# A two-block transformer kernel: first modulation columns loaded once, block 2's recurrence and norms rewritten, more buffers for the first query weights

## The chip, the cores and the metric

The kernel runs on one NeuronCore of a Trainium2 chip, as one launch. The metric is the device time of that launch in microseconds. Engines are named as in the profile: PE is TensorE's matmul, PEld its weight load, DVE VectorE, ACT ScalarE, POOL GpSimd, SP SyncE, which here only issues DMAs.

## What is computed

256 tokens `x` and 256 context tokens, 1024 wide, all fp32, pass a first block of two layers, a final norm, and a second block of one layer. Cut to what matters:

```python
for l in range(2):                                   # first block
    m_x = split6(silu(c) @ w_mod[l] + b_mod[l])      # shift, scale, gate, twice
    m_c = split6(silu(c_ctx) @ w_mod[l] + b_mod[l])
    h  = rmsnorm(x, g1) * (1 + m_x[1]) + m_x[0];  hc = same of ctx with m_c
    x  = x + m_x[2] * token_mix(h, kv of hc)         # attention, Fourier mix, pool mix
    h2 = rmsnorm(x, g2) * (1 + m_x[4]) + m_x[3]
    x  = x + m_x[5] * peer(h2)                       # 8 heads, top 16 of 128x128 experts
    if l == 0: ctx likewise
x = rmsnorm(x, final_g)
# second block
h = rmsnorm(x, norm1_g_2) * (1 + scale1) + shift1
x = x + gate1 * (attention(h), rwkv7_both_directions(h)) @ w_out
x = x + gate2 * peer(rmsnorm(x, norm2_g_2) * (1 + scale2) + shift2)
```

`peer` takes the 16 best of the sums of two key scores per head, so 128 experts for each token, reads the two 1024-wide rows of each expert, and adds the second, weighted with gelu of the token's product with the first.

## The kernel before

The program is first recorded and ordered, then issued. `Prog` (line 361) records every operation with the tile that it writes; `emit` (line 1803) writes the program down in segments (`x0`, `m0`, `p0`, `c0`, `q0` and so on), each with a span of due values in the table `ORDER`. `schedule` (line 558) then takes operations engine by engine, by what is ready, by priority (`lift` raises it) and due value, and assigns on-chip memory to tiles; a table `QUOTA` says how many buffers a tag (segment name and tile name, as `p0w`) may have at once. `replay` issues the result, so every operation stands at line 694 in the profile, and an edit of a number in a table can move operations everywhere. Each engine executes its own queue in order.

The streams, in the order of time: `x0` (first layer's mix of the tokens), `p0` (lookup and experts of the tokens), `c0` (mix of the context), `q0` (its experts), `x1` and `y1` (second layer's mix), `p1` (its experts), `b2` (final norm and block 2's mix), `p2` (its experts). The 256 tokens of an expert stage are two tiles of 128. For each tile 128 indirect DMAs on POOL fetch, for each of 128 tokens, one expert's two rows (8 KB, so 1.05 MB for a DMA, the `tab` transfers); DVE takes the products (`scalar_tensor_tensor` over 1024 columns with a running sum, and a `DVE_READ_ACCUMULATOR` behind it), ACT the gelu, and DVE or PE adds the weighted rows.

- Modulation. `load_c` (788) broadcasts `c`, applies silu; `mods` (795) loads a 128x1024 tile of transposed weights per column of 128 outputs and lets DVE multiply and sum it. `FIRST` is the list of the 16 columns that the first norm needs (8 scales, 8 shifts). At lines 1852 and 1856 they are loaded for `c`, and later again for `c_ctx`. `gscale` (817) makes (1 + scale) * g, eight operations of one column.
- Norms. `ln` (841): ACT squares, PE sums them with a matrix of ones, `rstd` (824) takes a logarithm and an exponential on ACT, DVE multiplies, ACT adds the shift. `final_norm` (1686) is followed by block 2's first `ln` (1923), both by token tile.
- Lookup. `select` loads query weights `wpq` (16 tiles of 0.5 MB) as tile `w` of its stream: `p0w` in the first.
- Recurrence. `wkv` (1551) is called for 4 groups of 2 heads in 2 directions. In chunks of 64 tokens, two to a tile `i`, it inverts a triangular matrix by five levels of products (line 1616), `Tm` and `XX` in turn, applies it to `Wr`, which gives `N`, and makes for each of four chunks the transition `GZ` and the input `HZ` of the state.

```python
1616            for lv in range(1, 6):
...
1638            nc.scalar.activation(N[:, i], px[:, :T].rearrange("p (e t) -> p e t", t=P), AF.Copy, scale=-1.0)
```

Of the kernel before, what the change touches and what calls it, by code (L numbers as in the profile page):

```python
# [17 lines left out]
OP = mybir.AluOpType  # L18
# [678 lines left out]
class Kern:  # L697
# [70 lines left out]
    def setup(self):  # L768
        nc, A = self.nc, self.A
        self.xT = self.t([P, KD, T], "xT", 1)  # L770
        self.cols = self.t([P, _NCOLS], "cols", 1)
        nc.sync.dma_start(self.xT, A["xT"])
        nc.sync.dma_start(self.cols, A["cols"])
        self.ident = self.t([P, P], "ident", 1)
        nc.sync.dma_start(self.ident, A["ident"])
        self.ones = self.t([P, P], "ones", 1)
        nc.vector.memset(self.ones, 1.0)
        self.eps = self.t([P, 4], "eps", 1)
        for i, v in enumerate((EPS, LNX_EPS, 0.0, 1.0)):
            nc.vector.memset(self.eps[:, i:i + 1], v)  # L780
        self.junk = self.t([P, D], "junk", 1, BF16)
        self.iota = self.t([P, P], "iota", 1)
        nc.gpsimd.iota(self.iota, pattern=[[1, P]], base=0, channel_multiplier=0,
                       allow_small_or_imprecise_dtypes=True)
        self.zero = self.t([P, 512], "zero", 1)
        nc.vector.memset(self.zero, 0.0)

    def load_c(self, dst, src):
        nc = self.nc
        nc.sync.dma_start(dst, src.to_broadcast([P, D]))  # L790
        s = self.t([P, D], "cs", 2)
        nc.scalar.activation(s, dst, AF.Sigmoid)
        nc.vector.tensor_tensor(dst, dst, s, op=OP.mult)

    def mods(self, wt, cols, outs, bufs=6):

        vec, left = self.nc.vector, {}
        for j in cols:
            left[j // 8] = left.get(j // 8, 0) + 1
        for j in cols:  # L800
            w = self.w(wt[j], "wm", bufs)
            left[j // 8] -= 1
            for m, cb, b in outs:
                vec.scalar_tensor_tensor(self.junk, w, 1.0, cb, op0=OP.mult, op1=OP.mult, accum_out=m[:, j:j + 1])
            if not left[j // 8]:
                c = slice(j // 8 * 8, j // 8 * 8 + 8)
                for m, cb, b in outs:
                    vec.tensor_tensor(m[:, c], m[:, c], b[:, c], op=OP.add)

# [7 lines left out]
    def gscale(self, m, j, g, name):  # L817
        r = self.t([P, KD], name, bufs=2)
        for k in range(KD):
            self.nc.vector.scalar_tensor_tensor(r[:, k:k + 1], m[:, j + k:j + k + 1], 1.0, g[:, k:k + 1],  # L820
                                                op0=OP.add, op1=OP.mult)
        return r
# [728 lines left out]
    def wkv(self, m, d, ld, a, R, Kf, kk, ka1, Vt, yT):  # L1551
# [29 lines left out]
        GZ = self.t([P, 4, 64], "GZ")  # L1581
        HZ = self.t([P, 4, 64], "HZ")
        te = [ch * 64 + (63 if d == 0 else 0) for ch in range(4)]
        ps = self.ps()
# [11 lines left out]
        for i in range(NT):  # L1596
# [18 lines left out]
            nc.vector.tensor_tensor(XX[:, :, 1], idb, al[:, 0], op=OP.subtract)  # L1615
            for lv in range(1, 6):
                px = self.ps()
# [5 lines left out]
                for e in range(2):  # L1623
                    if lv < 5:
                        nc.tensor.matmul(px[:, e, 0], XX[:, e, 1], Tm[:, e], start=True, stop=True)
                    nc.tensor.matmul(px[:, e, 1], Tm[:, e], XX[:, e, 1], start=True, stop=True)
                if lv < 5:
                    nc.vector.tensor_tensor(XX, XX, px, op=OP.subtract)
# [7 lines left out]
            for e in range(2):  # L1636
                nc.tensor.matmul(px[:, e * P:(e + 1) * P], XX[:, e, 1], Wr[:, i, e], start=True, stop=True)
            nc.scalar.activation(N[:, i], px[:, :T].rearrange("p (e t) -> p e t", t=P), AF.Copy, scale=-1.0)
            pr = self.ps()
# [9 lines left out]
            else:  # L1649
                nc.vector.tensor_tensor(yT[:, ts], pr[:, P:2 * P], yT[:, ts], op=OP.add)  # L1650
            pg = [self.ps() for _ in range(2)]
            for e in range(2):
                o = 64 * e
                for cc in range(2):
                    rs = slice(64 * cc, 64 * cc + 64)
                    nc.tensor.matmul(pg[cc][o:o + 64, :64], N[rs, i, e, :64], QKt[rs, 0, i, o:o + 64], start=True, stop=True)
                    nc.tensor.matmul(pg[cc][o:o + 64, 64:P], QKt[rs, 1, i, o:o + 64], Vt[rs, i, o:o + 64], start=True, stop=False)
                    nc.tensor.matmul(pg[cc][o:o + 64, 64:P], QKt[rs, 0, i, o:o + 64], N[rs, i, e, 64:], start=False, stop=True)
            for cc in range(2):
                ch = 2 * i + cc  # L1660
                nc.vector.tensor_tensor(GZ[:, ch], pg[cc][:, :64], self.id2, op=OP.add)
                nc.scalar.activation(HZ[:, ch], pg[cc][:, 64:P], AF.Copy, scale=Dc[:, te[ch]:te[ch] + 1])

        order = range(4) if d == 0 else range(3, -1, -1)
        Z = None
# [20 lines left out]
    def final_norm(self, xT, g):  # L1686
# [7 lines left out]
        nc.lift = self.lift  # L1694


FIRST = [j + k for k in range(KD) for j in (KD, 0)]
# [18 lines left out]
QUOTA = {  # L1716
# [78 lines left out]
ORDER.update({  # L1795
# [7 lines left out]
def emit(K, out, stage=None):  # L1803
# [45 lines left out]
    for q, n in zip(cbs, ("c", "c_ctx")):  # L1849
        K.load_c(q, A[n])  # L1850
    both = [(modx[0], cbs[0], bm[0]), (modc[0], cbs[1], bm[0])]
    K.mods(A["wmod0"], FIRST, both[:1])
    K.load_mix(0)
    h = norm1(xT, modx[0], 0)
    K.kvproj(0, h, T, True)
    K.mods(A["wmod0"], FIRST, both[1:])
    hc = K.ln(cT, K.gscale(modc[0], 8, n1[0], "gsc"), modc[0][:, 0:8], name="c")
# [54 lines left out]
    if stage == "peer1":  # L1912
        return dump(xT)
    K.final_norm(xT, K.col("final_g"))
    if stage == "first":
        return dump(xT)
    block2(K, out, stage, m2)


def block2(K, out, stage, m2):  # L1920
    nc, A, xT = K.nc, K.A, K.xT
    K.begin("b2", {"ps": 6, "pt": 2}, "b2", "p1s")
    h = K.ln(xT, K.gscale(m2, 8, K.col("norm1_g_2"), "gsc"), m2[:, 0:8], spans=TILES)
    if stage is None:
# [184 lines left out]
```

## Time and profile before

| | |
|---|---|
| runs | 3940.00, 3948.54, 3950.16 us; median 3948.54 |
| profiled execution | 3951.66 us, span 3949.7 us |
| granted TensorE clock | 0.887 of full speed |
| busy | PE 2966.0 (75%), PEld 1760.1, DVE 2858.3 (72%), ACT 1992.4 (50%), POOL 1485.3 us |
| DMA | 1314.31 MB, mean 333 GB/s |

The profile is of one execution. Busy times are shares of the whole span; the span has stages with different limits, so the rows below are mostly of single stretches. In a row of a timeline the brackets hold the idle time of that engine just before and what released it; in a grouped row stand count, busy time, mean length of one in ns, and idle time. A fp32 matmul leaves two rows, xN counts rows.

### The profile page before, as it was taken

How to read it: one execution, taken by the hardware profiler on the slowest of the kernel's cores; microseconds unless marked ns; L12 is line 12 of the kernel's file. 1: busy time of each engine (PE TensorE's matmuls, PEld its weight loads, DVE VectorE, ACT ScalarE, POOL GpSimd, SP SyncE). 2: the span in 40 equal slices, each digit the busy share in tenths (PEclk: the TensorE clock that was granted, in tenths of full speed). 3: DMA queues.
4: the chain of work that ended last, by engine and by line, in shares of the span. 5: the costliest groups of instructions: out<-in, count | busy, mean ns of one | idle time of the engine just before them, and what ended most of it. 6: DMA issues, size and time to landing. Idle time of an engine off the chain costs nothing.

```text
span 3949.7 us, 40304 instructions
## 1 busy us (share of the span) xinstructions
PE 2966.0 (75%) x10928; PEld 1760.1 (45%) x10928; DVE 2858.3 (72%) x6792; ACT 1992.4 (50%) x6181; POOL 1485.3 (38%) x1165
## 2 busy tenths in 40 slices
PE   5998844787895699866789656656989989666655
PEld 4767511454561256522376212212666776322222
DVE  5964999767799965576678986665644439986666
ACT  4123655556556676566536667666424234433322
POOL 0001345344343544455113455552201213564454
PEclk8999976898998899998899888887988999988887
DMA  8843999999999999999779999997520118999998
GB/s 330 299 153 113 369 374 387 383 406 375 388 398 397 411 404 412 418 421 420 253 264 397 416 403 421 421 422 291 195 82 19 37 45 340 410 419 421 422 422 356
DMA packets 222274, 1314.31 MB, mean 333 GB/s; under 512 B 24608, under 2 KB 29152, under 8 KB 90720
## 3 DMA queue, kind: packets, MB, share of 16 engines
q0 software_dynamic: 147456, 1073.81, 66.4%
q1 hardware_dynamic: 74592, 237.93, 16.5%
q8 instruction: 88, 1.44, 0.1%
q14 instruction: 138, 1.13, 0.1%
HBM read 1310.59 MB, written 1.05 MB: 332 GB/s over the span
## 4 chain that ended last, share of the span: by engine, by line
DVE 24%; issue 20%; POOL 15%; PE 15%; DMA 14%; ACT 4%; POOLq 0%; DVEq 0%; SPq 0%; ACTq 0%
DVE sb L694 24%; POOL sb L694 15%; PE bank L694 15%; DMA sb<-in_tab_dram,sb 11%; ACT sb L694 2%; ACT L694 1%; DMA sb<-in_wada_dram 1%; DMA sb<-in_wmod_dram 1%; DMA sb<-in_wo_dram 1%; POOLq L694 0%; DMA sb<-in_win_dram 0%; DMA sb<-in_wpq_dram 0%; DVEq L694 0%; SPq L694 0%; DVEq L2104 0%
## 5 line engine op out<-in xcount | busy, mean ns | idle before, releaser
L694 PE MATMUL bank<-sb 128*128 128x256 f32 (+8 forms) x10928 | 2966.0, 428 | 977.4 <-ACT sb L694 907.7
L694 PEld LDWEIGHTS bank<-sb 128*128 128x128 f32 (+5 forms) x10928 | 1760.1, 196 | 2182.9 <-ACT sb L694 1353.3
L694 DVE SCALAR_TENSOR_TENSOR sb<-sb 128x1024 f32<-128x1024 f32 (+4 forms) x1874 | 2073.0, 1133 | 708.4 <-DMA sb<-in_tab_dram,sb 551.2
L694 ACT ACTIVATE sb<-sb 128x1 f32<-128x1 f32 (+3 forms) x5336 | 1603.9, 308 | 1289.4 <-DVE sb L694 1109.8
L694 POOL DMA_INDIRECT sb<-in_tab_dram,sb x1024 | 1363.6, 1332 | 1569.0 <-PE bank L694 808.7
L694 ACT ACTIVATE sb<-bank 128x256 f32<-128x256 f32 (+5 forms) x458 | 182.9, 414 | 351.3 <-PE bank L694 315.3
L694 POOL TENSOR_TENSOR sb<-sb 128x256 f32<-128x256 f32 x128 | 113.5, 909 | 596.7 <-DVE sb L694 426.7
L694 DVE TENSOR_TENSOR sb<-sb 128x32 f32<-128x32 f32 (+12 forms) x934 | 273.6, 322 | 8.0 <-ACT sb L694 4.5
L694 ACT ACTIVATE sb<-bank,sb 128x256 f32<-128x256 f32 (+3 forms) x223 | 104.2, 475 | 291.5 <-PE bank L694 190.4
L694 ACT ACT_TABLE_LOAD x100 | 128.3, 1283 | 14.8 <-DMA sb<-in_c_dram 6.0
L694 DVE TENSOR_TENSOR sb<-bank,sb 128x512 f32<-128x512 f32 (+5 forms) x180 | 72.1, 421 | 84.7 <-PE bank L694 74.5
L694 DVE SCALAR_TENSOR_TENSOR sb<-bank,sb 128x128 f32<-128x128 f32 (+3 forms) x186 | 64.0, 380 | 92.2 <-PE bank L694 51.1
L694 POOL MEMSET sb<- 128x1024 f32 x8 | 7.7, 959 | 271.9 <-issue 153.3
L694 DVE TENSOR_TENSOR sb<-sb,bank 128x512 f32<-128x512 f32 (+1 forms) x96 | 56.4, 595 | 67.2 <-PE bank L694 64.8
L694 DVE DVE_READ_ACCUMULATOR sb<-sb 128x1 f32 x1232 | 101.3, 82 | 0.0
L694 DVE FIND_INDEX8 sb<-sb 128x8 uint32<-128x128 f32 (+1 forms) x384 | 96.3, 258 | 0.0
L694 DVE MAX8 sb<-sb 128x8 f32<-128x128 f32 (+1 forms) x384 | 85.0, 255 | 12.7 <-ACT sb L694 12.4
L694 DVE TENSOR_SCALAR sb<-sb 128x1 f32<-128x1 f32 (+7 forms) x232 | 50.0, 225 | 41.1 <-PE bank L694 17.3
L694 DVE TENSOR_REDUCE sb<-sb 128x16 f32<-128x800 f32 (+3 forms) x120 | 74.6, 634 | 1.2 <-issue 0.9
L694 DVE SCALAR_TENSOR_TENSOR sb<-sb,bank 128x256 f32<-128x256 f32 (+1 forms) x88 | 30.8, 369 | 32.7 <-PE bank L694 25.6
L694 DVE MATCH_REPLACE8 sb<-sb 128x128 f32<-128x128 f32 (+1 forms) x192 | 46.4, 249 | 0.0
L694 DVE MATCH_VALUE_LOAD sb<-sb 128x8 f32 x576 | 45.6, 79 | 0.0
(14 smaller groups left out, 95.2 us busy)
## 6 DMA issues: line engine op xcount, KB each, us to landing
sb<-in_win_dram SPq DMA_DIRECT2D x116, 512.0 KB
sb<-in_wmod_dram SPq DMA_DIRECT2D x112, 512.0 KB
sb<-in_wpq_dram SPq DMA_DIRECT2D x64, 512.0 KB
sb<-in_wada_dram SPq DMA_DIRECT2D x48, 512.0 KB
sb<-in_wout_dram SPq DMA_DIRECT2D x32, 512.0 KB
sb<-in_tab_dram,sb POOLq DMA_INDIRECT x1024
sb<-in_wo_dram SPq DMA_DIRECT2D x48, 256.0 KB
sb<-in_poolm_dram SPq DMA_DIRECT2D x6, 512.0 KB
```

Source lines behind the costliest of these rows:

```text
L694: getattr(getattr(nc, op.eng), op.meth)(*[res(x) for x in op.args], **{k: res(x) for k, x in op.kw.items()})
```

## The change

It does six things. (1) `c` and `cols` are loaded with priority, the 16 columns of `FIRST` get a segment `f0` with 16 buffers, are loaded once, and DVE goes over them first for `c`, then for `c_ctx`. (2) `gscale` is one operation over eight columns. (3) In `wkv` the inversion stops after four levels, and the last factor is applied to the result instead: `Y`, one more product, and `N = (...) - Y` on DVE. (4) `GZ` and `HZ` of the last chunk and `GZ` of the first in the order of the recurrence are left out, since they are not used. (5) `final_ln` takes both sums of squares from the same tokens, x squared and (x g) squared, and gets the second root from the first; block 2's `h` is made from the tokens themselves, and the final norm's scaling of them follows. (6) `p0w` has 14 buffers.

```diff
         self.cols = self.t([P, _NCOLS], "cols", 1)
         nc.sync.dma_start(self.xT, A["xT"])
+        nc.lift = 20
         nc.sync.dma_start(self.cols, A["cols"])
+        nc.lift = 0
...
-    def load_c(self, dst, src):
+    def load_c(self, dst, src, lift=0):
+
         nc = self.nc
+        nc.lift += lift
         nc.sync.dma_start(dst, src.to_broadcast([P, D]))
+        nc.lift -= lift
...
-    def mods(self, wt, cols, outs, bufs=6):
-
-        vec, left = self.nc.vector, {}
+    def mods(self, wt, cols, outs, bufs=6, apart=False):
+
+
+        vec = self.nc.vector
+
+        def one(w, j, m, cb):
+            vec.scalar_tensor_tensor(self.junk, w, 1.0, cb, op0=OP.mult, op1=OP.mult, accum_out=m[:, j:j + 1])
+
+        def bias(q, m, b):
+            c = slice(q * 8, q * 8 + 8)
+            vec.tensor_tensor(m[:, c], m[:, c], b[:, c], op=OP.add)
+
+        left = {}
         for j in cols:
             left[j // 8] = left.get(j // 8, 0) + 1
+        if apart:
+            ws = [self.w(wt[j], "wm", bufs) for j in cols]
+            for m, cb, b in outs:
+                for w, j in zip(ws, cols):
+                    one(w, j, m, cb)
+                for q in left:
+                    bias(q, m, b)
+            return
...
-        for k in range(KD):
-            self.nc.vector.scalar_tensor_tensor(r[:, k:k + 1], m[:, j + k:j + k + 1], 1.0, g[:, k:k + 1],
-                                                op0=OP.add, op1=OP.mult)
+        self.nc.vector.scalar_tensor_tensor(r, m[:, j:j + KD], 1.0, g[:, :KD], op0=OP.add, op1=OP.mult)
         return r
...
+        order = range(4) if d == 0 else range(3, -1, -1)
...
-            for lv in range(1, 6):
+            for lv in range(1, 5):
...
                 for e in range(2):
-                    if lv < 5:
+                    if lv < 4:
                         nc.tensor.matmul(px[:, e, 0], XX[:, e, 1], Tm[:, e], start=True, stop=True)
                     nc.tensor.matmul(px[:, e, 1], Tm[:, e], XX[:, e, 1], start=True, stop=True)
-                if lv < 5:
+                if lv < 4:
...
-            nc.scalar.activation(N[:, i], px[:, :T].rearrange("p (e t) -> p e t", t=P), AF.Copy, scale=-1.0)
+
+            Y = self.t([P, 2, P], "Tm", bufs=3)
+            nc.scalar.activation(Y, px[:, :T].rearrange("p (e t) -> p e t", t=P), AF.Copy)
+            px = self.ps()
+            for e in range(2):
+                nc.tensor.matmul(px[:, e * P:(e + 1) * P], al[:, 5, e], Y[:, e], start=True, stop=True)
+            Tm = self.t([P, 2, P], "Tm", bufs=3)
+            nc.scalar.activation(Tm, px[:, :T].rearrange("p (e t) -> p e t", t=P), AF.Copy)
+            px = self.ps()
+            for e in range(2):
+                nc.tensor.matmul(px[:, e * P:(e + 1) * P], XX[:, e, 1], Tm[:, e], start=True, stop=True)
+            nc.vector.tensor_tensor(N[:, i], px[:, :T].rearrange("p (e t) -> p e t", t=P), Y, op=OP.subtract)
...
-            pg = [self.ps() for _ in range(2)]
-            for e in range(2):
-                o = 64 * e
-                for cc in range(2):
-                    rs = slice(64 * cc, 64 * cc + 64)
-                    nc.tensor.matmul(pg[cc][o:o + 64, :64], N[rs, i, e, :64], QKt[rs, 0, i, o:o + 64], start=True, stop=True)
-                    nc.tensor.matmul(pg[cc][o:o + 64, 64:P], QKt[rs, 1, i, o:o + 64], Vt[rs, i, o:o + 64], start=True, stop=False)
-                    nc.tensor.matmul(pg[cc][o:o + 64, 64:P], QKt[rs, 0, i, o:o + 64], N[rs, i, e, 64:], start=False, stop=True)
             for cc in range(2):
                 ch = 2 * i + cc
-                nc.vector.tensor_tensor(GZ[:, ch], pg[cc][:, :64], self.id2, op=OP.add)
-                nc.scalar.activation(HZ[:, ch], pg[cc][:, 64:P], AF.Copy, scale=Dc[:, te[ch]:te[ch] + 1])
-
-        order = range(4) if d == 0 else range(3, -1, -1)
+                n = order.index(ch)
+                if n == 3:
+                    continue
+
+                pg = self.ps()
+                rs = slice(64 * cc, 64 * cc + 64)
+                for e in range(2):
+                    o = 64 * e
+                    nc.tensor.matmul(pg[o:o + 64, 64:P], QKt[rs, 1, i, o:o + 64], Vt[rs, i, o:o + 64], start=True, stop=False)
+                    nc.tensor.matmul(pg[o:o + 64, 64:P], QKt[rs, 0, i, o:o + 64], N[rs, i, e, 64:], start=False, stop=True)
+                    if n:
+                        nc.tensor.matmul(pg[o:o + 64, :64], N[rs, i, e, :64], QKt[rs, 0, i, o:o + 64], start=True, stop=True)
+                if n:
+                    nc.vector.tensor_tensor(GZ[:, ch], pg[:, :64], self.id2, op=OP.add)
+                nc.scalar.activation(HZ[:, ch], pg[:, 64:P], AF.Copy, scale=Dc[:, te[ch]:te[ch] + 1])
...
+    def final_ln(self, xT, g, gsc, sh):
+
+
+        nc = self.nc
+        hT = self.t([P, KD, T], "hT", bufs=1)
+        gg = self.t([P, KD], "gg", 1)
+        nc.vector.tensor_tensor(gg, g, gsc, op=OP.mult)
+        for u, v in TILES:
+            self.ahead(u)
+            n = v - u
+            pss = [self.ps()[:, :n] for _ in range(2)]
+            for k in range(KD):
+                for j in range(2):
+                    sq = self.t([P, T], "sq", bufs=3)[:, :n]
+                    nc.scalar.activation(sq, xT[:, k, u:v], AF.Square, scale=g[:, k:k + 1] if j else 1.0)
+                    nc.tensor.matmul(pss[j], self.ones, sq, start=(k == 0), stop=(k == KD - 1))
+            r = self.t([P, T], "rstd")[:, :n]
+            self.rstd(r, pss[0], D)
+            q = self.t([P, T], "rstd")[:, :n]
+            nc.vector.tensor_tensor(q, r, pss[1], op=OP.mult)
+            nc.vector.tensor_tensor(q, q, r, op=OP.mult)
+            self.rstd(q, q, D)
+            nc.vector.tensor_tensor(q, q, r, op=OP.mult)
+            for k in range(KD):
+                h = hT[:, k, u:v]
+                nc.vector.scalar_tensor_tensor(h, xT[:, k, u:v], gg[:, k:k + 1], q, op0=OP.mult, op1=OP.mult)
+                nc.scalar.activation(h, h, AF.Identity, bias=sh[:, k:k + 1])
+            for k in range(KD):
+                x = xT[:, k, u:v]
+                nc.vector.scalar_tensor_tensor(x, x, g[:, k:k + 1], r, op0=OP.mult, op1=OP.mult)
+        nc.lift = self.lift
+        return [hT]
...
-    'm1wm': 3, 'n1wm': 3,
+    'f0wm': 16, 'm1wm': 3, 'n1wm': 3,
...
-'p0w': 6,
+'p0w': 14,
...
+    'f0': (0, 2),
...
-        K.load_c(q, A[n])
+        K.load_c(q, A[n], 20 if n == "c" else 0)
     both = [(modx[0], cbs[0], bm[0]), (modc[0], cbs[1], bm[0])]
-    K.mods(A["wmod0"], FIRST, both[:1])
+    K.begin("f0", {}, "f0")
+    K.mods(A["wmod0"], list(range(8, 16)) + list(range(8)), both, 16, True)
+    K.begin("x0", MIX0, "x0")
     K.load_mix(0)
     h = norm1(xT, modx[0], 0)
     K.kvproj(0, h, T, True)
-    K.mods(A["wmod0"], FIRST, both[1:])
...
-    K.final_norm(xT, K.col("final_g"))
     if stage == "first":
+        K.final_norm(xT, K.col("final_g"))
...
-    h = K.ln(xT, K.gscale(m2, 8, K.col("norm1_g_2"), "gsc"), m2[:, 0:8], spans=TILES)
+    gsc = K.gscale(m2, 8, K.col("norm1_g_2"), "gsc")
+    if stage in ("mix2", "b2"):
+        h = K.ln(xT, gsc, m2[:, 0:8], spans=TILES)
+    else:
+        h = K.final_ln(xT, K.col("final_g"), gsc, m2[:, 0:8])
```

The order shifts with it. SyncE's queue at the program's start, before (`wmod` modulation weights, `win` the mix's first weights, `xT` and `cT` tokens and context):

```order
L694 DMA sb<-in_xT_dram 128x2048
L694 DMA sb<-in_c_dram 128x1024
L694 DMA sb<-in_wmod_dram 128x1024
L694 DMA sb<-in_cT_dram 128x2048
L694 DMA sb<-in_wmod_dram 128x1024 x4
L694 DMA sb<-in_cols_dram 128x324
L694 DMA sb<-in_win_dram 128x1024
L694 DMA sb<-in_c_ctx_dram 128x1024
L694 DMA sb<-in_win_dram 128x1024 x4
```

and after:

```order
L694 DMA sb<-in_c_dram 128x1024
L694 DMA sb<-in_cols_dram 128x324
L694 DMA sb<-in_xT_dram 128x2048
L694 DMA sb<-in_wmod_dram 128x1024 x8
L694 DMA sb<-in_cT_dram 128x2048
L694 DMA sb<-in_wmod_dram 128x1024 x8
L694 DMA sb<-in_win_dram 128x1024
L694 DMA sb<-in_c_ctx_dram 128x1024
L694 DMA sb<-in_win_dram 128x1024 x6
```

`cols` moves from the sixth row to the second, and 16 weight tiles stand together, with `cT` between, ahead of the first `win`.

GpSimd's queue from the first gather on, before (`in_tab` rows are gathers, `TENSOR_TENSOR` rows additions of the context's mix):

```order
L694 MEMSET sb 128x1024 x2
L694 DMA sb<-in_tab_dram,sb 128x2048 x125
L694 TENSOR_TENSOR sb<-sb 128x256
L694 DMA sb<-in_tab_dram,sb 128x2048 x7
L694 TENSOR_TENSOR sb<-sb 128x256
L694 DMA sb<-in_tab_dram,sb 128x2048 x8
L694 TENSOR_TENSOR sb<-sb 128x256
L694 DMA sb<-in_tab_dram,sb 128x2048 x6
L694 TENSOR_TENSOR sb<-sb 128x256
```

and after:

```order
L694 MEMSET sb 128x1024 x2
L694 DMA sb<-in_tab_dram,sb 128x2048 x40
L694 TENSOR_TENSOR sb<-sb 128x256
L694 DMA sb<-in_tab_dram,sb 128x2048 x4
L694 TENSOR_TENSOR sb<-sb 128x256
L694 DMA sb<-in_tab_dram,sb 128x2048 x6
L694 TENSOR_TENSOR sb<-sb 128x256
L694 DMA sb<-in_tab_dram,sb 128x2048 x8
L694 TENSOR_TENSOR sb<-sb 128x256
```

The first addition stands behind 40 gathers instead of 125.

ScalarE's queue at block 2's first norm, before (an operation that reads a bank is a logarithm, the rows of several are squares and shifts with an exponential ahead of them):

```order
L694 ACT_TABLE_LOAD
L694 ACTIVATE sb<-bank_68,sb 128x128
L694 ACT_TABLE_LOAD
L694 ACTIVATE sb<-sb 128x128 x12
L694 ACT_TABLE_LOAD
L694 ACTIVATE sb<-bank_65,sb 128x128
L694 ACTIVATE sb<-sb 128x128
L694 ACT_TABLE_LOAD
L694 ACTIVATE sb<-sb 128x128 x13
L694 ACT_TABLE_LOAD
L694 ACTIVATE sb<-bank_63,sb 128x128
L694 ACT_TABLE_LOAD
```

and after:

```order
L694 ACTIVATE sb<-sb 128x128 x23
L694 ACT_TABLE_LOAD
L694 ACTIVATE sb<-bank_69,sb 128x128
L694 ACTIVATE sb<-sb 128x128
L694 ACT_TABLE_LOAD
L694 ACTIVATE sb<-sb 128x128
L694 ACT_TABLE_LOAD
L694 ACTIVATE sb<-sb 128x128
L694 ACT_TABLE_LOAD
L694 ACTIVATE sb<-sb 128x128 x9
```

Six table loads before, with 12 and 13 operations between, become four, behind 23 shifts and squares in a row.

## Rows read from the trace of the kernel before

**Rows 1.** Busy time by engine, stretch by stretch, of the whole span

```profile
core 0: us, PE busy (x) PEld busy (x) DVE busy (x) ACT busy (x) POOL busy (x), PEclk, DMA share, GB/s
0.00:50.00 50.00, 9.53 (x32) 6.86 (x32) 24.26 (x52) 18.36 (x30) 0.43 (x5) 0.73 0.99 383
50.00:373.00 323.00, 300.64 (x1599) 240.79 (x1600) 213.70 (x519) 83.72 (x191) 11.54 (x10) 0.96 0.52 188
373.00:724.00 351.00, 191.08 (x538) 106.80 (x538) 330.22 (x921) 199.60 (x662) 156.08 (x117) 0.76 0.96 380
724.00:1120.00 396.00, 329.78 (x1183) 220.09 (x1182) 289.16 (x510) 231.33 (x780) 166.26 (x131) 0.91 0.96 383
1120.00:1900.00 780.00, 585.62 (x1653) 311.76 (x1652) 585.15 (x1359) 507.93 (x1659) 370.29 (x283) 0.92 1.01 412
...
2867.00:3222.00 355.00, 338.26 (x2182) 253.05 (x2182) 158.35 (x397) 117.97 (x283) 58.39 (x78) 0.91 0.14 44
```

**Rows 2.** Timeline of VectorE, first 75 us: start, length, operation, idle time ahead

```profile
16.91 0.18 DVE L694 TENSOR_SCALAR sb<-sb 128x24 f32<-128x24 f32 x1 [15.33 <-DMA sb<-in_cols_dram]
...
32.32 1.23 DVE L694 SCALAR_TENSOR_TENSOR sb<-sb 128x1024 bf16<-128x1024 f32 x1 [6.34 <-DMA sb<-in_wmod_dram]
...
41.28 1.23 DVE L694 SCALAR_TENSOR_TENSOR sb<-sb 128x1024 bf16<-128x1024 f32 x1 [2.61 <-DMA sb<-in_wmod_dram]
...
49.04 5.16 DVE L694 SCALAR_TENSOR_TENSOR sb<-sb 128x1 f32<-128x1 f32 x17
```

**Rows 3.** Timeline of TensorE, first 90 us

```profile
50.31 30.35 PE L694 MATMUL bank<-sb 128*128 128x256 f32 x132 [31.84 <-ACT sb L694]
```

**Rows 4.** The page's costliest groups and DMA queues

```profile
q0 software_dynamic: 147456, 1073.81, 66.4%
...
L694 ACT ACT_TABLE_LOAD x100 | 128.3, 1283 | 14.8 <-DMA sb<-in_c_dram 6.0
```

**Rows 5.** Timeline of SyncE's queue, 300 to 480 us

```profile
382.10 21.49 SPq L694 DMA_DIRECT2D sb<-in_wpq_dram  x4
...
407.39 17.93 SPq L694 DMA_DIRECT2D sb<-in_wpq_dram  x4
```

**Rows 6.** Two short stretches, columns as in rows 1

```profile
300.00:350.00 50.00, 48.69 (x375) 41.25 (x374) 13.75 (x54) 14.85 (x41) 1.90 (x2) 1.00 0.13 43
...
1180.00:1200.00 20.00, 10.90 (x15) 4.13 (x16) 20.00 (x69) 13.10 (x45) 9.79 (x8) 0.57 1.01 422
```

**Rows 7.** VectorE by operation and shape, 373 to 724 us

```profile
L694 DVE TENSOR_TENSOR sb<-sb 128x800 f32<-128x800 f32 x30 | 29.6, 985 | 0.1
L694 DVE FIND_INDEX8 sb<-sb 128x8 uint32<-128x128 f32 x60 | 16.6, 286 | 0.0
L694 DVE TENSOR_REDUCE sb<-sb 128x16 f32<-128x800 f32 x15 | 14.7, 980 | 0.0
```

**Rows 8.** Timeline of GpSimd, 365 to 1130 us

```profile
499.79 1.92 POOL L694 DMA_INDIRECT sb<-in_tab_dram,sb  x1 [7.91 <-DVE sb L694]
...
754.85 0.73 POOL L694 TENSOR_TENSOR sb<-sb 128x256 f32<-128x256 f32 x1
```

**Rows 9.** Timeline of all engines, 2734 to 2766 us

```profile
2739.26 0.83 ACT L694 ACTIVATE sb<-sb 128x128 f32<-128x128 f32 x3 [3.63 <-DVE sb L694]
...
2742.32 1.28 ACT L694 ACT_TABLE_LOAD   x1
...
2744.00 1.28 ACT L694 ACT_TABLE_LOAD   x1
...
2760.80 5.37 PE L694 MATMUL bank<-sb 128*128 128x256 f32 x13 [2.90 <-ACT sb L694]
```

**Rows 10.** TensorE by operation and shape, 2867 to 3222 us

```profile
L694 PE MATMUL bank<-sb 128*128 128x128 f32 x1102 | 194.0, 303 | 9.9 <-ACT sb L694 5.4 <-DVE sb L694 3.7
...
L694 PE MATMUL bank<-sb 64*64 64x64 f32 x536 | 54.7, 249 | 4.4 <-ACT sb L694 3.5 <-DVE sb L694 0.9
```

**Rows 11.** VectorE by operation and shape, 2867 to 3222 us

```profile
L694 DVE TENSOR_TENSOR sb<-sb,bank 128x512 f32<-128x512 f32 x56 | 38.0, 686 | 52.8 <-PE bank L694 50.4 <-ACT sb L694 1.5 <-issue 0.8
```

More of the change, by code (lines that the diff above doesn't have):

```diff
@@ L803, in mods @@
             for m, cb, b in outs:
-                vec.scalar_tensor_tensor(self.junk, w, 1.0, cb, op0=OP.mult, op1=OP.mult, accum_out=m[:, j:j + 1])
+                one(w, j, m, cb)
             if not left[j // 8]:
-                c = slice(j // 8 * 8, j // 8 * 8 + 8)
                 for m, cb, b in outs:
-                    vec.tensor_tensor(m[:, c], m[:, c], b[:, c], op=OP.add)
+                    bias(j // 8, m, b)
     def load_cb2(self):
```

4 rows, old and new, of the table QUOTA are left out of this document.

## The prediction, made before the changed kernel was timed

> **What bounds the kernel now.** I read the stretches first, because the share of busy time hides five stages with different limits. [rows 1] gives, for each stretch, TensorE's busy time (first figure, with its instruction count), then weight loads, VectorE, ScalarE and GpSimd, the granted clock, the DMA share and GB/s. Until 50 us the DMA engines are full (0.99, 383 GB/s) while TensorE works 9.5 us. From 50 to 373 us TensorE is busy 300.6 of 323 us with the DMA at 0.52: this stretch ends when TensorE has done its work. From 373 to 1900 us experts are gathered at 380, 383 and 412 GB/s, and VectorE is busy 330 of 351 us in the first of the three, 289 of 396 in the second: the DMA bounds it, VectorE nearly as much at its start. From 2867 to 3222 us, block 2's recurrence, TensorE is busy 338 of 355 us. Then I went to the rows where the edits lie.
>
> At the start, VectorE stands 15.33 us for `cols`, which lies behind five weight tiles in SyncE's queue, and twice more for modulation weights (6.34 and 2.61 us); the 17 rows of `gscale`'s one-column operations begin at 49.04 [rows 2]. TensorE has been idle 31.84 us when it starts at 50.31, released by ScalarE [rows 3].
>
> **A. The first columns: −14 us.** 16 tiles of 0.524 MB are loaded once instead of twice; `c` and `cols` come first. Ahead of the sixteenth column's landing stand `c` 0.52, `cols` 0.17, `xT` and `cT` 1.05 each and 16 tiles, 8.4: 11.2 MB, at the 383 GB/s that the first 50 us show (start included) 29.2 us. A column costs VectorE 1.27 us (five between 32.32 and 41.28, less the 2.61 idle [rows 2]), no more than the load of one (0.524 MB at that rate, 1.37 us), so VectorE ends some 1.5 us behind the last, at 31. But ScalarE's order has the sigmoid of `c_ctx` ahead of the eight biases that write `h`. `c_ctx` is behind one more tile: 12.2 MB, 31.9 us; a table load of 1.28 [rows 4], a pass over 1024 columns like VectorE's 1.23 and the bias put TensorE's start at 35 to 37. I take 36.3, 14 us before 50.31. Bounds: 11.2 MB at 422 GB/s with nothing in ScalarE's way would be 21 us; if VectorE waits for weights as before, 9 us more, 5 us. What is late next is the context's `h`: its 16 columns stand behind, 16 × 1.27 = 20.3 us, until about 57 to 59. By the order TensorE has 52 matmuls until there; a matmul leaves two rows, 132 of them in 30.35 us [rows 3], so 0.46 us each and 24 us, and it hardly waits. From there on TensorE has the same 734 matmuls before the first gather, and a stretch busy 300.6 of 323 us passes an earlier start on. The 16 dropped reloads themselves (8.4 MB at a DMA share of 0.52) give nothing more, as `gscale` doesn't at the six other norms.
>
> **B. Query weights and a new order of the gathers: −4 us.** Before, four wpq loads take 21.49 us to be issued, waiting for buffers, and four more 17.93, both with gathers under way [rows 5]. With 14 buffers at most 8 more tiles, 4.2 MB, can go ahead of the gathers, where between 300 and 350 us the DMA moved 43 GB/s, instead of into a stretch which at its best shows 422 GB/s [rows 6]: at most 10 us. But the edit re-plans the stretch. The first context addition on GpSimd comes after 40 gathers instead of 125, with seven more among the next 48, and the last lookups of the first tokens' second tile come after 72 gathers instead of 110. In the first 351 us the lookups' 128x800 products and 128-wide index searches cost VectorE 29.6 + 16.6 us, their sums 14.7 [rows 7]; 38 of 110 gathers' worth of these 61 us comes earlier, 21 us, and VectorE had just 21 us free there. So the gathers up to about the 110th may run up to 21 us late. The bytes do not grow: 512 gathers of 1.05 MB (1073.81 MB by 1024 [rows 4]) and some 70 MB of weights in 1527 us; at 422 GB/s they would take 1437, so 90 us lie in rates under the best, and spreading the context's weights over more gathers can win some back: 35 us of the 90 lie in the first stretch (351 × (1 − 380/422)). Bounds: −30 and, by the first rival's wait, +53. I take −4, nearest to the one sure item, the bytes moved ahead, less half for VectorE's lateness.
>
> **E1. One pass for two norms: −7 us.** Before, the first square of the second tile runs at 2739.26 and block 2's first matmul starts at 2760.80 [rows 9]: a norm, eight scalings, a second norm, and the first tile's root still behind. Now both sums of squares are taken from the same tokens, 16 squares in about 0.38 us each (eight took from 2739.26 to 2742.3): to 2745.3. Two roots follow, each a logarithm and an exponential with a load of 1.28 us before either: 4 × 1.28 + 4 × 0.38 (a logarithm fills the 0.40 us between the end of the load at 2742.32 and the load at 2744.00), two small products between and the last ones behind, 1.5 us in all: some 2753.5. That is 7 us; the first tile's part now runs under the gathers. Bounds −3 (the order puts something else there) and −12.
>
> Between logarithm and exponential the row at 2744.00 is a table load, as at 2742.32 before the logarithm [rows 9], so I count four loads, 5.1 us. The Trainium skill, page "ScalarE: Activation LUTs", section "Table sets: the hidden batching unit", has one set that holds both functions and prices a load at about 2.7 us: by it the two roots would cost one load, E1 would be near −9.5 us and the whole 2.4 us less. Here the rows decide, and they speak against it.
>
> **E2. Recurrence: −14 us.** Each of 16 rounds (8 calls, two tiles) has 2 fewer 128x128 matmuls, 28 for 30, and each call 8 fewer 64x64 ones, 16 for 24. That is 64 rows of 194.0/1102 = 0.176 us and 128 of 54.7/536 = 0.102 [rows 10], 11.3 + 13.1 = 24.4 us; the six groups of that view sum to 388.8 where TensorE was busy 338.3 [rows 1], so 21 us of time at most. At the other end, a round's chain of dependent steps keeps its 22 stages; one 128x512 subtraction of 0.69 us [rows 11] becomes a 128x256 one, some 0.3 us less, 5 us in 16 rounds. With TensorE at 95% the value lies nearer its own end: 14.
>
> **Sum.** −14 − 4 − 7 − 14 = −39 us. The profiled execution took 3951.7 us (span 3949.7), so 3912.7; it is 3.1 us above the median 3948.54, hence 3909.5.
>
> **Rivals.**
> 1. *GpSimd's order blocks the gathers; slower.* A gather behind a context addition can't be issued before that addition's input is there. Before, the first addition came so late that its row shows no idle time ahead of it [rows 8]; now eight stand among gathers 40 to 88, when the context's mix has 85 gathers less time to arrive. Price: a held-up gather stood 7.91 us [rows 8]; half of it counted, since gathers in flight go on meanwhile, 8 × 4 = 32, and VectorE's 21 us not caught up: +53 in B where the forecast has −4, 3966.5. It decides when the context's branch sums run more than three or four gathers (10 us) behind their place. For it: VectorE's 94%. Against it: TensorE is free there, 191 of 351 us [rows 1].
> 2. *Dependent steps bound the recurrence:* E2 −5, B 0, A and E1 as above: −26, 3922.5.
> 3. *Spread loads win back rate:* B −30: 3883.5. For it: 380 GB/s next to 422.
> 4. *The early start isn't passed on* since the context's columns or `win` tiles come late: A −3: 3920.5. For it: SyncE issues the 16 tiles before the first `win` tiles. Against: the DMA idles half of what follows.
>
> **How the numbers follow.** A measurement of this kernel tells about 0.3% (12 us) from no change, 3936.7 to 3960.4. Forecast 0.56, its parts' bounds about 3890 to 3928; rival 1 0.10, rival 2 0.12, rival 3 0.12, rival 4 0.10. Rivals 2 and 4 stay faster with 0.16 of their 0.22, since with B somewhat positive they come within 12 us of no change; rival 1 gives 0.08 slower and 0.02 same. Faster 0.56 + 0.12 + 0.16 = 0.84, same 0.06 + 0.02 = 0.08, slower 0.08. The range 3880 to 3936 takes in rivals 2, 3 and 4 and leaves out the slower case and the worst of the mixed ones, some 0.17.
>
> **What would show it.** Right: TensorE's long work starts at 35 to 37 us with no later wait over 4 us for a context column; the first gather 14 us earlier; the time from the first gather to the last of the context's 4 us shorter; block 2's first matmul 7 us nearer to the end of the gathers before it; the recurrence's stretch 14 us shorter. Wrong: GpSimd's additions with idle time ahead of them between gathers 40 and 88 and a DMA rate under 380 GB/s there, or a recurrence with more idle TensorE and the same length.

## The result and the profile after

| | before | after |
|---|---|---|
| median of 4 runs each, taken together | 3944.27 us | 3881.29 us |
| profiled execution's span | 3949.7 us | 3876.2 us |
| PE / DVE busy | 2966.0 / 2858.3 us | 2947.3 / 2846.9 us |
| DMA | 1314.31 MB | 1305.90 MB |

The ratio of the runs is 0.9837 (interval 0.9819 to 0.9855): 64 us less, where 39 were forecast. The sign was right and the median stands at the lower edge of the range; the change is 1.6 times the forecast one, and its terms were off in both directions.

The new kernel's stretches, cut where its own stages end (columns as in [rows 1]):

```profile
0.00:35.00 35.00, 10.99 (x32) 8.23 (x32) 24.97 (x55) 13.43 (x25) 0.43 (x5) 0.86 0.97 377
35.00:345.00 310.00, 295.86 (x1595) 237.50 (x1596) 210.10 (x489) 87.18 (x194) 11.36 (x11) 0.98 0.55 198
345.00:724.00 379.00, 312.00 (x1170) 214.96 (x1170) 342.08 (x991) 214.48 (x718) 150.23 (x119) 0.91 0.93 366
724.00:1120.00 396.00, 266.95 (x786) 155.49 (x784) 329.74 (x754) 234.65 (x783) 176.95 (x141) 0.78 0.98 398
1120.00:1855.00 735.00, 547.08 (x1412) 277.97 (x1413) 526.77 (x1015) 484.57 (x1584) 347.01 (x271) 0.87 1.01 415
...
2721.00:3155.00 434.00, 409.80 (x2470) 306.85 (x2469) 224.00 (x528) 164.50 (x364) 86.89 (x106) 0.94 0.26 84
```

What to see: TensorE's stretch before the gathers is 310 us long with 295.9 busy, where [rows 1] has 323 with 300.6. The table has the time between the marks that the prediction named, in both profiled executions. Each row starts where the one above ends, p1's gathers are counted to the last one's start, and the end is the issue of the output:

| from, to | before | after | difference | forecast |
|---|---|---|---|---|
| start, TensorE's long work | 50.3 | 35.4 | −14.9 | −14 |
| to the first gather | 322.8 | 309.5 | −13.3 | 0 |
| to the context's last gather | 1517.4 | 1509.7 | −7.7 | −4 |
| to the first p1 gather | 163.6 | 158.2 | −5.4 | 0 |
| p1's gathers | 666.4 | 669.2 | +2.8 | 0 |
| to block 2's `h` complete | 42.3 | 39.1 | −3.2 | −7 |
| to the end of its mixed heads | 467.7 | 433.6 | −34.1 | −14 |
| to the end | 715.0 | 716.7 | +1.7 | 0 |

The stretch from the context's last gather to p1's first was 155 to 167 us in the runs below, without a pattern in what was changed, so its −5 is scatter. The −8 of the gathers can't be told from scatter either: e10 and e11, whose order up to block 2 is that of the kernel before, took 1510.9 and 1509.2 us for them.

At the start, VectorE's timeline of the changed kernel answers to [rows 2] and TensorE's to [rows 3]; GpSimd's has the first gather:

```profile
5.47 0.18 DVE L694 TENSOR_SCALAR sb<-sb 128x24 f32<-128x24 f32 x1 [3.88 <-DMA sb<-in_cols_dram]
...
9.71 1.23 DVE L694 SCALAR_TENSOR_TENSOR sb<-sb 128x1024 bf16<-128x1024 f32 x1 [2.43 <-DMA sb<-in_wmod_dram]
...
33.88 3.46 ACT L694 ACTIVATE sb<-sb 128x1024 f32<-128x1024 f32 x7 [5.36 <-DMA sb<-in_c_ctx_dram]
...
35.39 24.63 PE L694 MATMUL bank<-sb 128*128 128x256 f32 x104 [7.17 <-ACT sb L694]
...
344.89 1.09 POOL L694 DMA_INDIRECT sb<-in_tab_dram,sb  x1 [37.48 <-DVE sb L694]
```

`cols` holds VectorE up for 3.88 us instead of 15.33, and the sigmoid of `c_ctx` stands at 33.88 on ScalarE, as reckoned.

### The profile page after: what moved, and what is told of

It is laid out like the page before. It is cut to its first block, busy times and chain, and to the rows that moved or that the text cites. A ratio compares the mean times of both kernels' runs of the same rounds, so it can differ in the third digit from the quotient of the medians.

```text
span 3876.2 us, 39736 instructions
## 1 busy us (share of the span) xinstructions
PE 2947.3 (76%) x10736; PEld 1744.7 (45%) x10736; DVE 2846.9 (73%) x6713; ACT 1990.8 (51%) x6173; POOL 1451.2 (37%) x1165
## 2 busy tenths in 40 slices
DMA packets 219968, 1305.90 MB, mean 337 GB/s; under 512 B 24352, under 2 KB 28896, under 8 KB 88416
## 4 chain that ended last, share of the span: by engine, by line
DVE 23%; issue 20%; PE 17%; DMA 15%; POOL 14%; ACT 3%; POOLq 0%; DVEq 0%; SPq 0%; ACTq 0%; another core or an unknown queue 0%
DVE sb L694 23%; PE bank L694 17%; POOL sb L694 14%; DMA sb<-in_tab_dram,sb 13%; ACT sb L694 2%; ACT L694 1%; DMA sb<-in_wada_dram 1%; DMA sb<-in_wmod_dram 0%; DMA sb<-in_win_dram 0%; DMA sb<-in_wo_dram 0%; POOLq L694 0%; DMA sb<-in_c_dram 0%; DMA sb<-in_wpq_dram 0%; SPq L694 0%; DVEq L694 0%
## 5 line engine op out<-in xcount | busy, mean ns | idle before, releaser
L694 PE MATMUL bank<-sb 128*128 128x256 f32 (+7 forms) x10736 | 2947.3, 432 | 922.0 <-ACT sb L694 862.5
L694 PEld LDWEIGHTS bank<-sb 128*128 128x128 f32 (+4 forms) x10736 | 1744.7, 197 | 2124.1 <-ACT sb L694 1308.1
L694 DVE SCALAR_TENSOR_TENSOR sb<-sb 128x1024 f32<-128x1024 f32 (+3 forms) x1804 | 2067.5, 1170 | 681.1 <-DMA sb<-in_tab_dram,sb 555.1
L694 ACT ACTIVATE sb<-sb 128x1 f32<-128x1 f32 (+4 forms) x5338 | 1602.0, 308 | 1256.3 <-DVE sb L694 1065.0
L694 POOL DMA_INDIRECT sb<-in_tab_dram,sb x1024 | 1330.7, 1300 | 1574.3 <-PE bank L694 776.7
L694 DVE TENSOR_TENSOR sb<-sb 128x800 f32<-128x800 f32 (+12 forms) x939 | 276.6, 324 | 13.2 <-ACT sb L694 8.7
L694 DVE TENSOR_TENSOR sb<-sb,bank 128x512 f32<-128x512 f32 (+2 forms) x82 | 46.5, 569 | 72.0 <-PE bank L694 58.4
L694 DVE TENSOR_SCALAR sb<-sb 128x128 f32<-128x128 f32 (+7 forms) x232 | 49.3, 223 | 24.3 <-PE bank L694 11.4
```

What stands on the lines that cost most here:

```text
L694: getattr(getattr(nc, op.eng), op.meth)(*[res(x) for x in op.args], **{k: res(x) for k, x in op.kw.items()})
```

## The experiments

The ratio is that to the kernel before, with its interval; differences in us are worked out from two ratios and 3948 us. "First gather" and the like are times in the profiled execution.

**e1: 6 buffers for the first query weights.** In the changed kernel:

```diff
-'p0w': 14,
+'p0w': 6,
```

> The changed kernel with 6 buffers for the first query weights again, all else kept; by its order the context's additions go back to behind 127 gathers. Theory (the buffers and the new order shorten only the stretch from the first gather to the context's last): first gather within 4 us of 345 us, first to last gather back from 1510 to 1514 to 1522 us, block 2 as in the changed kernel, total 4 to 12 us above it. Rival (the query weights that are loaded early also shorten the stretch before the first gather, beyond the 14 us of the early start): the first gather comes 8 us or more later, at 353 or behind.

Ratio 0.9880 (0.9858 to 0.9903), 17 us more than the changed kernel. First gather at 353.4, first to last gather 1510.5. The rival holds: the buffers shorten the stretch ahead of the gathers, from TensorE's start 317.6 us here and 309.5 with 14, and TensorE waits 6.8 us for `win` instead of 1.1. The order of `win` and modulation loads in SyncE's queue changes with the buffers. The gathers are no longer than with 14; where the other half of the 17 us lies is open.

**e2: the reloads back.** The 16 columns of `c_ctx` are loaded again behind the first norm.

```diff
-    K.mods(A["wmod0"], list(range(8, 16)) + list(range(8)), both, 16, True)
+    K.mods(A["wmod0"], list(range(8, 16)) + list(range(8)), both[:1], 16, True)
...
+    K.mods(A["wmod0"], FIRST, both[1:])
     hc = K.ln(cT, K.gscale(modc[0], 8, n1[0], "gsc"), modc[0][:, 0:8], name="c")
```

> The changed kernel with the 16 first columns of c_ctx loaded a second time, as before; c, cols and the token columns stay first with 16 buffers. Theory (the reloads in SyncE's queue held up the mix's weights, and so cost TensorE more waits until the first gather): TensorE still starts at 35 to 37 us, but the first gather comes 8 to 14 us later than 345 us, with waits of TensorE for win or VectorE back. Rival (the early start alone shortened this stretch, and the rest of the 28 us is from elsewhere): the first gather within 3 us of 345 us.

Ratio 0.9925 (0.9905 to 0.9946), 35 us more. TensorE starts at 35.52, and the first gather still comes at 373.3, no earlier than before. The timelines of TensorE and SyncE of this run, and ten microseconds of it by engine:

```profile
35.52 21.56 PE L694 MATMUL bank<-sb 128*128 128x256 f32 x86 [7.03 <-ACT sb L694]
69.74 1.22 PE L694 MATMUL bank<-sb 128*128 128x256 f32 x2 [12.66 <-DMA sb<-in_win_dram]
...
43.48 15.11 SPq L694 DMA_DIRECT2D sb<-in_wmod_dram  x16
59.54 1.62 SPq L694 DMA_DIRECT2D sb<-in_win_dram  x2
```

```profile
60.00:70.00 10.00, 0.26 (x1) 0.26 (x2) 9.55 (x17) 0.21 (x1) 0.00 (x0) 0.56 1.03 409
```

And the same ten in the kernel before:

```profile
60.00:70.00 10.00, 10.00 (x48) 8.22 (x47) 5.48 (x10) 3.49 (x5) 0.00 (x0) 1.00 1.02 390
```

The 16 reloads stand ahead of `win` in SyncE's queue, the DMA is full, and TensorE works 0.26 of 10 us. In the changed kernel the same ten microseconds have 9.24 busy at a DMA share of 0.60. The theory holds, and more strongly than expected: with the reloads the whole of the early start is lost. This wait belongs to the new order, though. In the kernel before the DMA is as full, but TensorE, which starts later, works 10.00 of these 10 us; its queue has `win` tiles among the reloads.

**e3: two norms again.** `final_norm` and then `ln`, as before.

> The changed kernel with the final norm and block 2's first norm as two passes again. Theory (the shared pass gains less than the 7 us predicted, since the first tile's 16 products stand ahead of the second tile's in VectorE's queue): from the last p1 gather to the first of p2 3 to 5 us longer than the changed kernel's 517 us. Rival (as predicted): 7 us longer or more.

Ratio 0.9841 (0.9815 to 0.9866), no difference in total. From p1's last gather to p2's first it is 526.1 us, 9.5 more than in the changed kernel, which by the words of the expectation is the rival; but half of that lies behind the norm, in the recurrence (438.3 for 433.6 us), which this edit leaves as it is. From the last p1 gather to `h` it is 44.0 us, for 39.1. Over all runs, six with two norms have 42.3 to 47.2 (mean 44.3), seven with the shared pass, e8 not among them, 38.3 to 42.6 (mean 40.3). So the norm itself differs by 4 us, the size that the theory gave, too little to be seen in the total. The place on the four engines in the changed kernel, which answers to [rows 9]:

```profile
2701.77 4.29 DVE L694 SCALAR_TENSOR_TENSOR sb<-sb 128x128 f32<-128x128 f32 x16
...
2705.98 2.15 DVE L694 SCALAR_TENSOR_TENSOR sb<-bank,sb 128x128 f32<-128x128 f32 x8
2706.36 4.65 ACT L694 ACTIVATE sb<-sb 128x128 f32<-128x128 f32 x15 [1.75 <-DVE sb L694]
...
2711.03 1.28 ACT L694 ACT_TABLE_LOAD   x1
...
2712.99 1.28 ACT L694 ACT_TABLE_LOAD   x1
...
2719.13 7.19 PE L694 MATMUL bank<-sb 128*128 128x256 f32 x14 [5.62 <-ACT sb L694]
```

The first tile's 16 products (2701.77) stand on VectorE ahead of the second tile's eight (2705.98): 4.2 us which I had placed under the gathers. A load stands between logarithm and exponential again (2712.99), four in all. The Trainium skill, page "ScalarE: Activation LUTs", section "Table sets: the hidden batching unit", has one set with both functions, by which one load would do for the pair; this trace disagrees, with a load of 1.28 us between them each time.

**e8: the scale vectors earlier,** `gsc` and `gg` in segment `n1`:

```diff
     K.mods2(m2, FIRST)
+    K.gsc2 = K.gscale(m2, 8, K.col("norm1_g_2"), "gsc")
+    K.gg = K.t([P, KD], "gg", 1)
+    nc.vector.tensor_tensor(K.gg, K.col("final_g"), K.gsc2, op=OP.mult)
```

> The changed kernel with block 2's scale vectors gsc and gg computed in the stage before (segment n1) instead of at block 2's start, so that the first tile's 16 products stand ahead of the last two additions of p1 in VectorE's queue. Theory (these 16 products, 4.3 us, are what the shared pass lost): from the last p1 gather to block 2's h 4 us shorter than the 38 to 40 us of the changed kernel, total 2 to 6 us less. Rival (they ran beside the wait for squares): no difference there.

Ratio 0.9848 (0.9829 to 0.9868), 42.8 us from the last p1 gather to `h`. A miss: the 16 products do move ahead of p1's last additions, but delay those. What would place them under the gathers was not found.

**e4: the old recurrence,** all of `wkv` as before.

> The changed kernel with the old recurrence: five levels, N on ScalarE, all GZ and HZ made. Theory (the removed matmuls are worth their full time where TensorE is busy 95%, 21 us, and the 13 us beyond that which the two traces show are TensorE's clock, which differs from run to run): the stretch from the last p1 gather to the first of p2 20 to 26 us longer than 517 us. Rival 1 (dependent steps bound it): 5 to 10 us longer. Rival 2 (the rest is a lasting effect of the recurrence's new order on clock and waits): 30 us longer or more.

Ratio 0.9901 (0.9879 to 0.9922), 25 us more; 549.6 us from p1's last gather to p2's first, 33 more. Rival 2: it is lasting, and more than the removed matmuls. So the two pieces were taken apart, in the changed kernel and in the one before.

**e6, e11: four levels alone,** all `GZ` and `HZ` made; e6 in the changed kernel, e11 in the one before:

```diff
-            for lv in range(1, 6):
+            for lv in range(1, 5):
...
+            nc.vector.tensor_tensor(N[:, i], px[:, :T].rearrange("p (e t) -> p e t", t=P), Y, op=OP.subtract)
```

> The changed kernel with the four-level inversion, but all GZ and HZ made as before. Theory (the removed matmuls count in full): of the 32 us between the old recurrence and the new one (466 and 434 us from block 2's h to its mixed output), the levels bring 11 us and their new order the end of the 6 us wait for win, so 446 to 456 us. Rival (dependent steps, the 128x512 subtraction that goes, are what counts): 440 or less.

> The kernel before, only with the four-level inversion. Theory (by itself it removes 32 matmuls of 128x128, 8 to 11 us, unless TensorE's clock falls more often in its order): mean granted clock times the stretch from block 2's h to its mixed output 5 to 11 us under that of before (434 us), whatever the stretch itself. Rival (it makes the chain of dependent steps longer in every order): that product as before or more.

Ratio 0.9962 (0.9945 to 0.9979) for e6, 49 us more than the changed kernel; 1.0062 (1.0044 to 1.0079) for e11, 24 us more than before. Theory and rival of e6 both fail: the stretch has 498 us, and 496 in e11. e11's product, given below, is 2 us under that of before, less than its theory's 5 to 11.

**e7, e10: the unused pieces dropped alone,** five levels as before; e7 in the changed kernel, e10 in the one before. The edit is the hunk with `if n == 3: continue`.

> The changed kernel with the old five levels, but without the unused GZ and HZ. Theory (the removed matmuls count in full): 64 matmuls of 64x64, 13 us, so 449 to 457 us from block 2's h to its mixed output, against 466 and 434. Rival (they ran in gaps of a chain of dependent steps): 462 or more, and the levels alone 440 or less.

> The kernel before, only without the unused GZ and HZ. Theory (this piece carries most of the recurrence's gain): from block 2's h to its mixed output 440 to 450 us instead of 468, total 16 to 28 us less. Rival (the gain in the changed kernel came from the order in which it happened to fall): 455 or more.

Ratio 0.9840 (0.9817 to 0.9864) for e7, the same as the changed kernel; 0.9941 (0.9923 to 0.9959) for e10, 23 us less than before. The stretch has 442.5 and 438.6 us, somewhat less than either theory. This piece carries nearly all of the recurrence's gain. One row for the stretch from `h` to the mixed heads of each kernel, before first, then e10, e11:

```profile
2763.00:3230.00 467.00, 437.95 (x2666) 326.14 (x2666) 231.19 (x537) 164.02 (x369) 87.53 (x106) 0.93 0.24 78
```

```profile
2756.00:3194.00 438.00, 408.64 (x2539) 309.85 (x2537) 227.38 (x521) 166.33 (x366) 85.57 (x105) 0.96 0.26 84
```

```profile
2754.00:3250.00 496.00, 464.92 (x2595) 341.89 (x2594) 227.71 (x537) 167.09 (x373) 86.43 (x106) 0.87 0.22 74
```

Read length times granted clock (the figure behind GpSimd's): 434 before, 420 in e10, 432 in e11, 408 in the changed kernel (434 × 0.94). By this measure, good to some 2 us since the clock is rounded, dropping the unused products is worth 14 us, and both pieces 26, close to the 13.1 and 24.4 us of [rows 10]; the levels give 2 alone and 12 together with the other. The order counts here too: e8 has the matmuls of the changed kernel in another order, and 440 us at 0.96, a product of 422. The rest of each difference is the clock: e11 has fewer matmuls than before (2595 rows for 2666), and TensorE is busy 27 us longer with them, at 0.87 instead of 0.93.

**e5: the order of `c` and `cols` as before,** columns loaded once.

```diff
-        nc.lift = 20
+        nc.lift = 0
         nc.sync.dma_start(self.cols, A["cols"])
...
-        K.load_c(q, A[n], 20 if n == "c" else 0)
+        K.load_c(q, A[n], 0)
```

> The changed kernel without the priority for c and cols: xT comes first again and cols behind the 16 tiles, but the columns are still loaded once. Theory (until about 70 us the DMA is the bound, and the bytes dropped from it are the gain, not the order in which c and cols come): TensorE's start moves by up to 6 us, the first gather by no more than 4 us from 345 us, total within 5 us of the changed kernel. Rival (the early c and cols carry a good part of the gain): the first gather 8 us or more later.

Ratio 0.9900 (0.9884 to 0.9915), 25 us more. VectorE and TensorE in this run:

```profile
31.12 0.18 DVE L694 TENSOR_SCALAR sb<-sb 128x24 f32<-128x24 f32 x1 [29.54 <-DMA sb<-in_cols_dram]
...
55.10 25.95 PE L694 MATMUL bank<-sb 128*128 128x256 f32 x106 [27.22 <-ACT sb L694]
```

My theory fails here: 0.17 MB behind 16 tiles of weights keep VectorE idle for 29.54 us. But from TensorE's start to the first gather it is 311.7 us, as in the changed kernel (309.5) and unlike before (322.8) or e2 (337.8). So the time of the first gather is a sum: a start that `c` and `cols` set, and a length that the reloads set, and the buffers by e1.

**e9: the first columns' part alone,** in the kernel before.

> The kernel before with the first columns' part alone: c and cols first, the 16 columns loaded once with 16 buffers; old norms, recurrence, scale vectors and 6 buffers for the query weights. Theory (two gains that need each other: TensorE starts 15 us earlier, and the dropped reloads take out its waits for win): TensorE's long work starts at 35 to 36 us, the first gather comes at 348 to 356 us, 17 to 25 us earlier than before, everything behind it as before, total 15 to 30 us less. Rival (it needs the 14 buffers too): the first gather at 360 or later.

First gather at 351.8, 21 us earlier, as expected, yet the ratio is 1.0006 (0.9994 to 1.0018): nothing is left of it. First to last gather takes 1534.5 us, where the kernel before, e10 and e11 take 1509 to 1517. A stretch of 100 us at the end of the tokens' gathers, in e9 and then in the changed kernel:

```profile
1152.00:1252.00 100.00, 73.36 (x246) 44.53 (x244) 99.97 (x418) 51.45 (x171) 31.98 (x28) 0.88 0.89 358
```

```profile
1145.00:1245.00 100.00, 58.00 (x82) 21.17 (x81) 100.00 (x252) 65.22 (x219) 54.42 (x40) 0.69 1.01 421
```

VectorE is full in both and works at the context's lookup, in e9 with 38 of its 128-wide index searches in this stretch, in the changed kernel with 12. In e9 28 GpSimd operations run for 40, GpSimd waits 44.9 us for TensorE (4.7 in the changed kernel), and the DMA falls to 358 GB/s; in the kernel before it moves 401 at the same distance from the first gather. The lookup's first search starts at 1127.85 in e9, 776 us behind the first gather and 25 us ahead of the tokens' last one (1153.2, by the program's order). In the kernel before this lead was 88 us (1101.21 to 1188.7), in the changed kernel 310 (970.40 to 1280.1).

**e12: the same with 14 buffers.**

> The kernel before with the first columns' part as in e9, and 14 buffers for the query weights; nothing else of the change. In e9 the first gather came 21 us earlier, but the gathers then took 17 us longer, since the context's lookup (q0) stood 48 us later behind the first gather than before, when hardly a gather of the tokens was left beside it. Theory (the 14 buffers move the context's mix and lookup forward, and with it the early start lasts): first gather at 345 to 348 us, first to last gather 1508 to 1514 us, total 25 to 40 us less than before. Rival (the loss in e9 is from something else, and the 14 buffers bring only the prologue): first to last gather 1525 us or more, total within 15 us of before.

Ratio 0.9897 (0.9877 to 0.9917), 41 us less than before: first gather at 347.02, as the theory has it; first to last gather 1506.1, which like the total lies a little beyond the theory's range, on the side away from the rival. Beside the columns the buffers are worth 43 us here, though not by what I had priced; no run has them alone. They aren't the only way: e1 has 6 and also takes 1510.5 us, in yet another order with a lead of 64 us. And the lead by itself doesn't set the length, since e2 has 119 us and takes 1522.3. That e9 lost its gain by the late lookup is argued from its stretch, not shown.

e12 and e10, −41 and −23 us, each known to some 8 us, together make the −64 of the change. No version of these is faster than the changed kernel by more than the intervals; e7 equals it without the four-level inversion.

## Why the prediction was wrong in size, by its own steps

- **A, the start: right.** 36.3 us forecast, 35.39 found; the sigmoid of `c_ctx` was the last wait, as named.
- **A, the reloads: the step that failed first.** I wrote that the 16 dropped reloads "give nothing more", since the DMA's mean share was 0.52 from 50 to 373 us. That mean hides full stretches: 1.02 from 60 to 70 us before, and 1.03 in e2, where `win` stands behind 8.4 MB, 20 us at 409 GB/s. The stretch from TensorE's start to the first gather is 13.3 us shorter where I had 0. The columns alone give about half of that (e9: 316.2 for 322.8 us), the 14 buffers the rest (309.5 and 311.4 in the changed kernel and e12, 317.6 and 316.2 with 6 buffers in e1 and e9); the halves are rough, since four runs with the changed kernel's order up to there have 305.7 to 312.1. And the early start passes on only because the reloads are gone: with them back it doesn't (e2, 28 us longer, my fourth rival's mechanism).
- **B: sum not told from scatter, grounds wrong.** The 129th gather stood 446 us behind the first, where it had been 390, so 56 us late and not the 21 that I had reckoned, with the DMA at 326 GB/s from 445 to 545 us; and everything was caught up at the 257th (792 for 802). Idle additions and a low rate are what I had named as the first rival's sign, and 56 is near its 53 us. But the additions on GpSimd waited 4.5 us at most and 11 in all, so its wait isn't what made the gathers late, and the time came back. What the 14 buffers did do is not what I had priced: they shorten the stretch ahead of the gathers, and beside the columns they undo the loss of e9 (43 us to e12).
- **E1: 7 us forecast, about 4 found.** Four loads, as the rows said; in the trace the first tile's 16 products stand in the way with 4.2 us, but no run shows the gain without them.
- **E2: mis-sized, 14 us forecast, 34 found** (some 31 between the means of all runs with the old and the new recurrence). I took a value between the matmuls' full 24.4 us and a 5 us bound from the chain of steps, and scaled the former to 21 because the groups' sum exceeded TensorE's busy time. By length times clock the removed matmuls were worth 26, near the full 24.4, and the chain's bound didn't hold it down; the other 7 or so are the clock, which no row of before priced. That the price came out is in part the luck of the order: the levels, 11.3 of the 24.4, gave 2 by themselves, and made the stretch 29 to 32 us longer (e11 against before, e6 against e4).
- In the profiled pair the miss is −35 us (−74 for −39): −13 from the stretch ahead of the first gather, −20 from E2, some −4 and −5 from the context's gathers and the stretch behind them, some +7 from E1, p1 and the rest. The medians, 63 us apart, put 11 us of the pair down to scatter.

## What to carry to other kernels

Cut a stretch where its bound changes, not where a label ends: a mean DMA share of 0.52 hid a full queue, and 16 loads in it ahead of the weights that TensorE needed next cost 28 us in e2. An earlier start is worth its time only if the next stage's work comes with it; check what the next lookup or load will find beside it. Where an engine is busy 95% of a stretch, the removed work's full price (24.4 us) was nearer to what came (26) than a chain's bound (5), but a new order can add to it or take it back by TensorE's clock. So test each piece of a rewrite by itself, since one of two may carry all of it: the four-level inversion, with fewer matmuls, gained nothing in total beside the other piece and lost 24 us without it.

## What the runs showed of the hardware

How much of TensorE's clock is granted went with what was changed in a stretch, and repeated: the recurrence with four levels alone had 0.87 in two different kernels (e6, e11), with the unused products dropped 0.95 and 0.96 (e7, e10). Four stretches of e11:

```profile
3160.00:3170.00 10.00, 10.00 (x77) 8.39 (x77) 5.86 (x13) 2.33 (x8) 2.14 (x3) 1.00 0.55 219
3170.00:3175.00 5.00, 2.03 (x15) 1.65 (x13) 0.37 (x1) 4.94 (x9) 3.58 (x6) 1.00 0.00 2
3175.00:3180.00 5.00, 4.30 (x24) 3.22 (x24) 4.50 (x11) 0.56 (x2) 2.86 (x4) 0.58 0.00 0
3180.00:3215.00 35.00, 35.00 (x138) 24.04 (x137) 6.59 (x17) 3.80 (x11) 1.29 (x2) 0.50 0.10 30
```

TensorE works 2.03 of 5 us, the grant falls to 0.50 (1.2 GHz), and stays there for 35 us in which TensorE never pauses. The waits in the whole recurrence are hardly longer than before (30 us of idle TensorE in e11, 27 before); why this order draws more falls from them was not settled.
